# Row-sum reciprocals spread by DMAs through DRAM in place of TensorE transposes, in a two-block transformer kernel

## Chip, cores and metric

One core of one Trainium2 chip runs the whole program in one launch. The metric is the device time of a run in microseconds (us), the median of the runs shown. TensorE is PE in the profile (its weight loads PEld), VectorE is DVE, ScalarE is ACT, GpSimd is POOL, and SyncE, whose queue issues every DMA of this kernel, is SP.

## What is computed

512 tokens of width 1024 pass through two blocks of two layers each. All data are fp32. Every layer of the first block has four attention branches (MLA, stick-breaking, forget-gate "fox", memory), every layer of the second has four others (dense, window with a sink, neighbourhood, differential). A branch has four heads of width 64, and its output is gated. Cut to the part that the change concerns:

```python
def _memory_attention(q, k, v):
    logits = jnp.einsum('bshd,bmhd->bhsm', q * (q.shape[-1] ** -0.5), k)
    p = jax.nn.softmax(logits, axis=-1).astype(v.dtype)
    return jnp.einsum('bhsm,bmhd->bshd', p, v)
...
for n in range(N_BRANCHES):                      # first block
    yb = branches[n].reshape(b, s, BRANCH_WIDTH) * jax.nn.silu(gate_z[:, :, n])
    merged = merged + merge_g[:, :, n] * (yb @ w_branch[n])
out = merged @ w_out
...
mix = jnp.concatenate([o_a * silu(g_a), o_b * silu(g_b), o_c * silu(g_c), o_d * silu(g_d)], axis=-1)
x = x + jnp.einsum('bsm,md->bsd', mix, w_out[l])  # second block
```

Each softmax is divided by the sum of its row, one number for each token and head. Stick-breaking has no such division.

## The kernel before, in words

Projections are kept feature-major: 128 partitions hold features, 512 columns the tokens. Each fp32 matmul is made of three fp32r matmuls on a high and a low part (`mm3`, lines 328 to 330; `split`, lines 319 and 322). Weights come in units of up to 128x1024: one DMA into one of three `raw` buffers (line 376), an ACT copy for the high part, a DVE subtraction for the low one, into three `wh`/`wl` buffers.

Heads are worked in pairs, two heads of 64 features to the 128 partitions. For each head and each block of 128 queries, PE makes the scores (`qk`, lines 512 and 513) and ACT the exponentials with the row sums in `accum_out` (`softmax`, line 534): so a pair's sums stand token-major, as 128 partitions x 2 heads x 4 blocks. PE transposes the probabilities into PSUM (`av`, line 552; the pool of `T` tiles has two buffers), ACT and DVE split them (`th`, `tl`), and PE multiplies by the values (lines 564 and 565) into a feature-major `O`, which `o_evac` (lines 592 and 593) adds into the pair's tile `o`.

The sums are token-major and `o` is feature-major, so the reciprocals have to be turned and spread. Before, `head_rep` does this: a DVE copy (line 617) widens the 128x8 reciprocals to `hrep`, 128x512 with every number 64 times, into a `tmp` buffer; four PE transposes (line 620) turn it into `rep`, 128x512, which takes one of the two `T` buffers in PSUM; DVE multiplies `o` by it (`do_finish`, line 634, or 632 and 636) and then the gate by `o` (line 639).

`recip` (line 652) makes the reciprocals as soon as a pair's second head is done, and `finish` puts the pair on a list, `pending`. The words of `ORDER1` and `ORDER2` say in which order the generators of the branches are advanced, and the word `f` takes the oldest pair off the list and runs `do_finish`. This gives the program's order. The framework's scheduler then orders each engine's instructions anew, within what dependencies and the rotation of buffers allow, so an instruction may stand far from its place in the code. A layer has eight pairs. In the first block six of them have reciprocals (memory, fox, MLA), in the second all eight. Differential attention (`diff_d`) has reciprocals that hold the RMS norm too (line 1417). `dense_a` calls `head_rep` once more for its keys, outside `finish`.

Pairs are finished in this order in the first block: memory 0, memory 1, fox 0, fox 1, MLA 0, MLA 1; in the second: differential 0, dense 0, dense 1, window 0, neighbourhood 0, differential 1, window 1, neighbourhood 1.

SP issues DMAs in its own fixed order and waits at the first that isn't ready. Among them are the weights, and the stacks of queries and keys of each pair (`move`, line 333: `qs`, `ks`, `hs`, `ls`, `kr`), whose parts are copied across partitions before `qk` can read them.

Of the kernel before, what the change touches and what calls it, by code (L numbers as in the profile page):

```python
# [9 lines left out]
F32 = mybir.dt.float32  # L10
# [8 lines left out]
S = 512  # L19
# [265 lines left out]
def half(e):  # L285
    return slice(64 * e, 64 * e + 64)
# [24 lines left out]
class Build:  # L311
# [308 lines left out]
            nc.tensor.transpose(rep[:, cols(tt)], b[:, tt].rearrange("p a b -> p (a b)"), self.ident)  # L620
        return rep

    def finish(self, *args, **kw):
        self.pending.append((args, kw))

    def do_finish(self, at, o, rc=None, g=None, perm=None):

        nc = self.nc
        if rc is not None:
            rep = self.head_rep(rc.rearrange("p e i -> p i e"))  # L630
            if perm:
                nc.vector.tensor_tensor(perm(o), perm(o), rep.rearrange("p (c r) -> p c r", r=8), ALU.mult)
            elif g is None:
                nc.vector.tensor_tensor(o, o, rep, ALU.mult)
            else:
                nc.vector.scalar_tensor_tensor(o, o, g, rep, ALU.mult, ALU.mult)
        self.gated.remove(at)
        self.done.add(at)
        nc.vector.tensor_tensor(self.z[at], self.z[at], o, ALU.mult)
# [16 lines left out]
    def setup(self):  # L656
        nc, tc, ctx = self.nc, self.tc, self.ctx
        pool = lambda n, b, **k: ctx.enter_context(tc.tile_pool(name=n, bufs=b, **k))
        self.cp = pool("const", 1)
        self.psp, self.pss, self.pst, self.pso = (pool(n, b, space=PSUM) for n, b in zip(("psp", "pss", "pst", "pso"), BANKS))  # L660
        self.rawp, self.wp = pool("raw", RAW), pool("wp", WP)
        self.smp = pool("small", 8)
        self.w_done, self.w_ready, self.wout, self.stp = 0, {}, None, None
        self.xs = [nc.dram_tensor(f"xs{i}", (S, DM), F32).ap() for i in range(3)]
        ct = self.cp.tile([128, NCONST], F32, name="ct")
        self.c = {k: ct[:, o : o + n] for k, (o, n) in COFF.items()}
        self.ident = self.c["ident"]
        big = lambda nm: self.cp.tile([128, 8, S], F32R, name=nm)
        self.zth, self.ztl = big("zth"), big("ztl")
        self.zp, self.z = pool("z", ZO), {}  # L670
        self.gated = set()
        nc.scalar.preload_act_table_set(EXPS)
        with tc.tile_pool(name="x0", bufs=1) as xp:
            x = xp.tile([128, 2, 8, 256], F32, name="x0")
            at = 0
            for n, (hf, k0, k1) in enumerate(X0):
                v = x[:, hf, k0:k1]
                c = slice(at, at + 256 * (k1 - k0))
                at = c.stop
                nc.sync.dma_start(v, self.ins["xt"][:, c].rearrange("p (k t) -> p k t", t=256))  # L680
                if n in W0:
                    self.w_prefetch(W0[n])
                self.split(*(t[:, k0:k1, cols(hf, 256)] for t in (self.zth, self.ztl)), v)
        self.w_prefetch(WP)
        nc.sync.dma_start(ct, self.ins["const"])
# [67 lines left out]
    def pools(self, n, st, tmp, pt, p, v):  # L753

        tc = self.tc
        left, right = ExitStack(), ExitStack()
        pool = lambda nm, b: right.enter_context(tc.tile_pool(name=f"{nm}{n}", bufs=b, side="right"))
        self.stp = left.enter_context(tc.tile_pool(name=f"st{n}", bufs=st, side="left"))
        self.pp, self.ptp, self.op, self.vp = pool("p", 1), pool("pt", pt), pool("o", OO), pool("v", v)
        self.tmpp, self.kp = pool("tmp", tmp), pool("k", 1)  # L760
        self.pb = p
        left.callback(lambda: setattr(self, "stp", None))
        return left, right

    def weave(self, order, l, **parts):

        self.pending, self.done = [], set()
        self.mcos = self.msin = self.qm = self.qs = self.krs = self.logf = self.vb = None
        parts = {k: iter(f(l)) for k, f in parts.items()}
        for word in order.split():  # L770
            name = word.rstrip("0123456789")
            for _ in range(int(word[len(name) :] or 1)):
                if name == "f":
                    args, kw = self.pending.pop(0)
                    self.do_finish(*args, **kw)
                else:
                    next(parts[name])
        assert not self.pending
        for name, p in parts.items():
            assert next(p, self) is self, name  # L780


    def layer1(self, l):
        left, right = self.pools(l, **POOLS1)
        with right:
            self.weave(ORDER1, l, first=self.first, mem=self.memory, sb=self.stick, mla=self.mla, misc=self.misc, fox=self.fox, g=self.gates1)
# [444 lines left out]


    def layer2(self, l):
        if 0 not in self.layers and l == self.layers[0] % 2:
            self.constants()
        if l == 0:
# [114 lines left out]
    def diff_d(self, l):  # L1351
# [34 lines left out]
        for pr in range(2):  # L1386
            ku = [unit(hl[2], cols(2 * pr + c, 32), (0, 1, 0, 1)) for c in range(2)]
            o, sm = self.new_o(), self.sums()
            for e in range(2):
# [16 lines left out]
                if e:  # L1406
# [8 lines left out]
                    nc.vector.tensor_scalar(v, v, RMS_EPS, None, ALU.add)  # L1415
                    rs = self.rsqrt(v.rearrange("p a b -> p (a b)")).rearrange("p (a b) -> p a b", a=2)
                    nc.vector.tensor_tensor(rc, rc, rs, ALU.mult)
                    self.finish(6 + pr, o, rc, g)
                yield

    def neigh_c(self, l):
# [59 lines left out]
```

## Time and profile before

| | |
|---|---|
| median of 3 runs | 1417.88 us (1415.82 to 1418.38) |
| the profiled execution | 1419.11 us, of which its span is 1417.3 us |
| PE busy | 1363.2 us, 96% of the span |
| DVE, ACT busy | 999.9 us (71%), 832.3 us (59%) |
| granted PE clock, mean | 0.986 of full speed |
| DMA packets' share of 16 engines | 37.8%, mean 113 GB/s |

The profile is one execution on the chip. A page gives busy times by engine, the chain of waits that ended last, and the costliest groups of instructions; a timeline gives single instructions with the idle time before them in brackets, with what ended it. An idle engine costs nothing unless it bounds the stage. A PE row's duration holds the drain of its pipeline, so what a row costs PE is read from its start to the next row's start.

### The profile page before, as it was taken

The page shows a single profiled execution, that of the slowest core. Times are in us where ns is not written, and L with a number is a line of the kernel's source. Part 1 is how long each engine was busy: PE and PEld are TensorE (multiplying, and loading weights), DVE is VectorE, ACT ScalarE, POOL GpSimd, SP SyncE. Part 2 cuts the span into 40 slices and gives each one's busy share as a digit, 9 for nine tenths or more (in the row PEclk, how much of TensorE's full clock was granted, in tenths as well). Part 3 has the DMA queues.
Part 4 walks back from the last instruction along what each step waited for, and adds up shares of the span by engine and source line. Part 5 has one row for each costly group of instructions (what it writes and reads, how often), then busy time and mean ns, then how long its engine had stood idle before and what let it go on. Part 6 is the DMA issues. An engine that isn't in the chain of part 4 may idle for free.

```text
span 1417.3 us, 20005 instructions
## 1 busy us (share of the span) xinstructions
PE 1363.2 (96%) x7112; PEld 1111.0 (78%) x7112; DVE 999.9 (71%) x2077; ACT 832.3 (59%) x1672; POOL 4.3 (0%) x12
## 2 busy tenths in 40 slices
PE   8999998999999999998999999999999999999998
PEld 7887786777789777877777788877777888877776
DVE  6666545898764776257989675887777575886785
ACT  5584547765413765476856243776866346667763
POOL 0000000000000000000000000000000000000000
PEclk9999999999999999999999999999999999999999
DMA  7534222213625424222135436323434265215241
GB/s 238 172 105 118 72 75 80 75 60 108 207 100 159 139 71 117 75 81 80 41 89 179 163 115 180 111 60 103 131 100 145 109 177 150 75 45 151 62 140 67
DMA packets 61266, 160.31 MB, mean 113 GB/s; under 512 B 11056, under 2 KB 11696, under 8 KB 61168
## 3 DMA queue, kind: packets, MB, share of 16 engines
q1 hardware_dynamic: 61168, 159.05, 37.8%
q8 instruction: 56, 0.92, 0.3%
q14 instruction: 42, 0.34, 0.1%
HBM read 117.92 MB, written 8.91 MB: 89 GB/s over the span
## 4 chain that ended last, share of the span: by engine, by line
PE 77%; ACT 8%; DVE 8%; DMA 4%; issue 2%; SPq 0%; DVEq 0%; ACTq 0%
PE proj L328 11%; PE proj L329 11%; PE proj L330 11%; PE T L552 3%; PE pso L328 3%; PE pso L329 3%; PE pso L330 3%; PE O L564 3%; PE O L565 2%; PE s L901 2%; PE projv L329 2%; PE projv L330 2%; PE projv L328 2%; PE projwb L329 2%; PE projwb L330 2%
## 5 line engine op out<-in xcount | busy, mean ns | idle before, releaser
L328 PE MATMUL proj<-zth,wh 128*128 128x512 f32 (+1 forms) x864 | 323.9, 375 | 9.5 <-ACT wh L319 5.8
L329 PE MATMUL proj<-ztl,wh 128*128 128x512 f32 (+1 forms) x864 | 323.4, 374 | 0.3
L330 PE MATMUL proj<-zth,wl 128*128 128x512 f32 (+1 forms) x864 | 322.9, 374 | 0.0
L322 DVE TENSOR_TENSOR wl<-raw,wh 128x1024 fp32r<-128x1024 f32 (+2 forms) x153 | 183.1, 1197 | 135.1 <-ACT wh L319 126.7
L319 ACT CAST wh<-raw 128x1024 fp32r<-128x1024 f32 (+2 forms) x153 | 157.6, 1030 | 170.4 <-PE proj L329 139.7
L328 PEld LDWEIGHTS proj<-zth,wh 128*128 128x128 f32 x864 | 164.1, 190 | 32.9 <-ACT wh L319 5.8
L330 PEld LDWEIGHTS proj<-zth,wl 128*128 128x128 f32 x864 | 164.2, 190 | 23.7 <-DVE wl L322 1.0
L329 PEld LDWEIGHTS proj<-ztl,wh 128*128 128x128 f32 x864 | 164.3, 190 | 22.8 <-DVE ztl L322 0.7
L322 DVE TENSOR_TENSOR tl<-T,th 128x512 fp32r<-128x512 f32 (+3 forms) x176 | 98.9, 576 | 28.3 <-ACT th L319 27.7
L552 PE MATMUL T<-ct,p 128*128 128x128 f32 x560 | 103.6, 279 | 9.9 <-ACT p L534 7.7
L319 ACT CAST th<-T 128x512 fp32r<-128x512 f32 (+3 forms) x176 | 85.5, 498 | 41.8 <-PE T L552 39.0
L552 PEld LDWEIGHTS T<-ct,p 128*128 128x128 f32 x560 | 71.1, 142 | 30.5 <-ACT p L534 11.3
L528 DVE TENSOR_REDUCE nm<-s 128x1 f32<-128x512 f32 (+1 forms) x128 | 77.5, 616 | 19.6 <-PE s L513 10.2
L534 ACT ACTIVATE p<-s,nm 128x512 f32<-128x512 f32 (+1 forms) x96 | 59.1, 619 | 17.3 <-DVE nm L528 16.7
L564 PE MATMUL O<-th,V 128*128 128x512 f32 (+3 forms) x176 | 62.4, 371 | 2.6 <-ACT th L319 2.2
L565 PE MATMUL O<-tl,V 128*128 128x512 f32 (+3 forms) x160 | 59.3, 376 | 5.0 <-DVE tl L322 4.8
L328 PE MATMUL pso<-wout,zth 128*128 128x512 f32 x128 | 51.7, 404 | 4.7 <-DVE y L1134 4.7
L328 PE MATMUL projv<-wh,zth 128*128 128x256 f32 (+1 forms) x192 | 55.0, 287 | 0.0
L330 PE MATMUL projv<-wh,ztl 128*128 128x256 f32 (+1 forms) x192 | 54.7, 285 | 0.0
L329 PE MATMUL projv<-wl,zth 128*128 128x256 f32 (+1 forms) x192 | 54.6, 284 | 0.0
L330 PE MATMUL projwb<-y,wl 128*128 128x512 f32 x128 | 51.6, 403 | 0.0
L328 PE MATMUL projwb<-y,wh 128*128 128x512 f32 x128 | 51.1, 399 | 0.2
(380 smaller groups left out, 2927.7 us busy)
## 6 DMA issues: line engine op xcount, KB each, us to landing
raw<-in_w_dram SPq DMA_DIRECT2D x173, 512.0 KB
xs<-y SPq DMA_DIRECT2D x12, 512.0 KB
ks<-hs SPq DMA_DIRECT2D x32, 128.0 KB
early<-xs SPq DMA_DIRECT2D x16, 256.0 KB
bias<-in_bias_dram SPq DMA_DIRECT2D x8, 448.0 KB
qs<-hs SPq DMA_DIRECT2D x24, 128.0 KB
qs<-ls SPq DMA_DIRECT2D x24, 128.0 KB
hs<-ls SPq DMA_DIRECT2D x24, 128.0 KB
```

What stands on the lines that cost most here:

```text
L319: self.nc.scalar.copy(h, src)
L322: self.nc.vector.tensor_tensor(l, src, h, ALU.subtract)
L328: self.nc.tensor.matmul(ps, ah, bh, start=i == 0, stop=False)
L329: self.nc.tensor.matmul(ps, ah, bl, start=False, stop=False)
L330: self.nc.tensor.matmul(ps, al, bh, start=False, stop=i == n - 1)
L528: nc.vector.tensor_reduce(nm, s, AX.X, ALU.max, negate=True)
L534: nc.scalar.activation(p[:, :w], src, AF.Exp, bias=nm, scale=sc, accum_out=sm)
L552: nc.tensor.transpose(T[:, cols(a)], P[i][:, c : c + 128], self.ident)
L564: nc.tensor.matmul(o[:, c], vsel(j), th[:, c], start=j == 0, stop=False)
L565: nc.tensor.matmul(o, vsel(j), tl[:, :w], start=False, stop=j == nk - 1)
L901: nc.tensor.matmul(z[:, c:w], m, x, start=False, stop=n == len(sums) - 1, skip_group_check=True)
```

## The change

`finish` counts the pairs that a layer still has to come. For all but the last one of a layer in the first block (`late = 1`) and the last two in the second (`late = 2`), if they have reciprocals, it issues three DMAs on SP at once: one writes the 128x8 reciprocals to a new DRAM tensor of 2x4x128, token order last (so each of the 1,024 numbers is a piece of four bytes), and two read a head's 512 numbers back, each row spread over 64 partitions, into `rep`, now an SBUF tile of a new pool of two buffers (`repp`). `do_finish` multiplies by this tile; the DVE copy and the four transposes are not made. 22 of the 28 pairs with reciprocals take this way: five in each layer of the first block, six in each of the second. The other six, and the keys of `dense_a`, keep `head_rep`.

```diff
-    def finish(self, *args, **kw):
-        self.pending.append((args, kw))
-
-    def do_finish(self, at, o, rc=None, g=None, perm=None):
+    def finish(self, at, o, rc=None, **kw):
+
+        self.to_finish -= 1
+        if rc is not None and self.to_finish >= self.late:
+            d = self.nc.dram_tensor(f"rc{self.nrc}", (2, 4, 128), F32).ap()
+            self.nrc += 1
+            with self.nc.allow_non_contiguous_dma(reason="few bytes"):
+                self.nc.sync.dma_start(d.rearrange("e i p -> p e i"), rc)
+            rep = self.repp.tile([128, S], F32, tag="rep", name="rep")
+            for e in range(2):
+                self.nc.sync.dma_start(rep[half(e)], d[e].rearrange("i p -> (i p)").partition_broadcast(64))
+            kw["rep"] = rep
+        self.pending.append(((at, o, rc), kw))
+
+    def do_finish(self, at, o, rc=None, g=None, perm=None, rep=None):
 
         nc = self.nc
         if rc is not None:
-            rep = self.head_rep(rc.rearrange("p e i -> p i e"))
+            if rep is None:
+                rep = self.head_rep(rc.rearrange("p e i -> p i e"))
...
-        self.tmpp, self.kp = pool("tmp", tmp), pool("k", 1)
+        self.tmpp, self.kp, self.repp = pool("tmp", tmp), pool("k", 1), pool("rep", 2)
...
-        self.pending, self.done = [], set()
+        self.pending, self.done, self.to_finish = [], set(), 8
...
     def layer1(self, l):
+        self.late = 1
...
     def layer2(self, l):
+        self.late = 2
```

Since `rep` no longer waits for a buffer of `T` and of `tmp`, the scheduler sets the multiplications elsewhere. Three places follow. Each comes twice in the program, once for each layer of its block, and the engine's rows are those of the first layer.

DVE, first block, memory attention, between the reciprocals of pair 0 and the low parts (`tl`) of pair 1's last head; before:

```order
L652 RECIPROCAL sums<-sums 128x8
L593 TENSOR_TENSOR o<-O,ot 64x512
L322 TENSOR_TENSOR tl<-T,th 128x512
L528 TENSOR_REDUCE nm<-s 128x1
L322 TENSOR_TENSOR tl<-T,th 128x512
L528 TENSOR_REDUCE nm<-s 128x1 x2
L593 TENSOR_TENSOR o<-O,ot 64x512
L322 TENSOR_TENSOR tl<-T,th 128x512 x2
L322 TENSOR_TENSOR wl<-raw,wh 128x1024
```

The same place now:

```order
L664 RECIPROCAL sums<-sums 128x8
L593 TENSOR_TENSOR o<-O,ot 64x512
L322 TENSOR_TENSOR tl<-T,th 128x512
L528 TENSOR_REDUCE nm<-s 128x1
L322 TENSOR_TENSOR tl<-T,th 128x512
L528 TENSOR_REDUCE nm<-s 128x1 x2
L593 TENSOR_TENSOR o<-O,ot 64x512
L646 TENSOR_TENSOR o<-o,rep 128x512
L322 TENSOR_TENSOR tl<-T,th 128x512 x2
L651 TENSOR_TENSOR z<-z,o 128x512
```

The multiplication by `rep` came much later before (after the fox rows and most of the stick-breaking); now it stands right behind the pair's last addition, ahead of two `tl` that PE needs.

DVE, second block, differential attention, behind the last step of pair 0's reciprocals (the first row); before:

```order
L1417 TENSOR_TENSOR sums<-sums,rs_y 128x8
L528 TENSOR_REDUCE nm<-s 128x1
L1402 TENSOR_SCALAR rl<-rl,nlam,sums 128x1
L528 TENSOR_REDUCE nm<-s 128x1
L1403 SCALAR_TENSOR_TENSOR p<-p_9412,rl,p 128x512
L322 TENSOR_TENSOR wl<-raw,wh 128x1024
L1401 RECIPROCAL rl<-s_9427 128x1
L528 TENSOR_REDUCE nm<-s 128x1
L1402 TENSOR_SCALAR rl<-rl,nlam,sums 128x1
L528 TENSOR_REDUCE nm<-s 128x1
L1403 SCALAR_TENSOR_TENSOR p<-p_9429,rl,p 128x512
L1401 RECIPROCAL rl<-s_9444 128x1
```

The same place now:

```order
L1431 TENSOR_TENSOR sums<-sums,rs_y 128x8
L528 TENSOR_REDUCE nm<-s 128x1
L1416 TENSOR_SCALAR rl<-rl,nlam,sums 128x1
L528 TENSOR_REDUCE nm<-s 128x1
L1417 SCALAR_TENSOR_TENSOR p<-p_9397,rl,p 128x512
L322 TENSOR_TENSOR wl<-raw,wh 128x1024
L1415 RECIPROCAL rl<-s_9412 128x1
L528 TENSOR_REDUCE nm<-s 128x1
L1416 TENSOR_SCALAR rl<-rl,nlam,sums 128x1
L528 TENSOR_REDUCE nm<-s 128x1
L1417 SCALAR_TENSOR_TENSOR p<-p_9414,rl,p 128x512
L648 SCALAR_TENSOR_TENSOR o<-o,subg,rep 128x512
```

Again the multiplication moved forward, to ten rows behind the reciprocals and ahead of the next softmax work of the same branch.

SP, first block, the stacks of fox's second pair; before:

```order
L333 DMA qs<-ls 64x512
L376 DMA raw<-in_w_dram 128x1024
L333 DMA hs<-ls 64x512
L333 DMA ls<-cqrows 4x512
L333 DMA ls<-hs 64x512
L333 DMA kr<-ckrows 4x512
L333 DMA kr<-ls 64x512
L333 DMA ks<-hs 64x512 x2
```

The same place now, with the DMAs of fox's first pair among them:

```order
L333 DMA qs<-ls 64x512
L376 DMA raw<-in_w_dram 128x1024
L630 DMA rc<-sums 128x8x1
L333 DMA hs<-ls 64x512
L333 DMA ls<-cqrows 4x512
L333 DMA kr<-ls 64x512
L633 DMA rep<-rc 64x512 x2
L333 DMA ls<-hs 64x512
L333 DMA kr<-ckrows 4x512
L333 DMA ls<-ckrows 4x512
L333 DMA ks<-hs 64x512 x2
```

The write waits for the reciprocals and the two reads wait for the write, and the stacks of the next pair stand behind both.

## Rows read from the trace of the kernel before

**Rows 1.** Page, part 1: busy time, share of the span, instructions.

```profile
PE 1363.2 (96%) x7112; PEld 1111.0 (78%) x7112; DVE 999.9 (71%) x2077; ACT 832.3 (59%) x1672; POOL 4.3 (0%) x12
```

**Rows 2.** Page, part 4: the chain that ended last, by engine.

```profile
PE 77%; ACT 8%; DVE 8%; DMA 4%; issue 2%; SPq 0%; DVEq 0%; ACTq 0%
```

**Rows 3.** Groups by line and form: busy us, mean ns, idle before and releasers.

```profile
L634 DVE TENSOR_TENSOR o<-o,rep 128x512 f32<-128x512 f32 x20 | 13.7, 683 | 6.1 <-PE rep L620 5.5
L617 DVE COPY hrep<-sums 128x512 f32<-128x512 f32 x28 | 11.6, 420 | 0.1
```

**Rows 4.** Timeline of PE: start us, duration us, instruction [idle before <- releaser].

```profile
157.09 0.50 PE L328 MATMUL proj<-zth,wh 128*128 128x512 f32 x1 [1.50 <-DVE cql L932]
...
278.81 0.63 PE L620 MATMUL rep<-ct,hrep 128*128 128x128 f32 x4
279.28 0.60 PE L552 MATMUL T<-ct,p 128*128 128x128 f32 x4
...
1014.12 0.60 PE L620 MATMUL rep<-ct,hrep 128*128 128x128 f32 x4
1014.47 0.36 PE L512 MATMUL s<-ks,qs 128*128 128x256 f32 x1
```

**Rows 5.** Timeline of PE, two pairs finished together in the second block.

```profile
1044.28 1.07 PE L620 MATMUL rep<-ct,hrep 128*128 128x128 f32 x8
1045.89 0.44 PE L552 MATMUL T<-ct,p 128*128 128x128 f32 x2 [0.54 <-DVE o L634]
1046.83 0.41 PE L552 MATMUL T<-ct,p 128*128 128x128 f32 x1 [0.51 <-DVE o L632]
...
1048.59 0.58 PE L565 MATMUL O<-tl,V 128*128 128x256 f32 x1 [0.70 <-DVE tl L322]
```

**Rows 6.** Busy us by stretch: length, PE, PEld, DVE, ACT, POOL, PEclk, DMA, GB/s.

```profile
1040.00:1060.00 20.00, 17.33 (x94) 13.69 (x92) 16.04 (x44) 11.31 (x29) 0.00 (x0) 0.83 0.42 111
1336.00:1356.00 20.00, 17.24 (x98) 13.69 (x97) 16.32 (x44) 11.97 (x31) 0.00 (x0) 0.91 0.46 141
```

**Rows 7.** Timeline of DVE behind the memory branch's first reciprocals.

```profile
96.36 0.19 DVE L652 RECIPROCAL sums<-sums 128x8 f32<-128x8 f32 x1
...
101.27 0.68 DVE L593 TENSOR_TENSOR o<-O,ot 64x512 f32<-64x512 f32 x1 [0.91 <-ACT ot L592]
102.87 1.29 DVE L322 TENSOR_TENSOR tl<-T,th 128x512 fp32r<-128x512 f32 x2 [0.91 <-ACT th L319]
```

**Rows 8.** Timeline of PE, the first reader of these `tl`.

```profile
103.92 0.39 PE L565 MATMUL O<-tl,mV 128*128 128x512 f32 x1
```

**Rows 9.** Timeline of DVE behind the differential branch's first reciprocals.

```profile
931.27 0.15 DVE L1417 TENSOR_TENSOR sums<-sums,rs_y 128x8 f32<-128x8 f32 x1
...
935.94 0.75 DVE L1403 SCALAR_TENSOR_TENSOR p<-p,rl,p 128x512 f32<-128x512 f32 x1
...
938.40 0.74 DVE L1403 SCALAR_TENSOR_TENSOR p<-p,rl,p 128x512 f32<-128x512 f32 x1
```

**Rows 10.** Timeline of PE, the reader of the last of these `p`.

```profile
939.85 0.38 PE L552 MATMUL T<-ct,p 128*128 128x128 f32 x2
```

**Rows 11.** Timeline of SP's DMA issues: start us, us on the queue.

```profile
80.55 1.11 SPq L333 DMA_DIRECT2D ks<-hl  x2
...
83.46 0.47 SPq L333 DMA_DIRECT2D hl<-hl  x1
...
226.05 0.46 SPq L333 DMA_DIRECT2D hs<-ls  x1
...
238.16 0.49 SPq L333 DMA_DIRECT2D hs<-hs  x1
```

**Rows 12.** The chain that ended last, in order of time: start us, us, what.

```profile
992.80 4.77 DMA hs<-hs
```

**Rows 13.** Page, part 3: DMA queue, packets, MB, share of 16 engines' time.

```profile
q1 hardware_dynamic: 61168, 159.05, 37.8%
```

**Rows 14.** The same view of 113.5 to 118.5 us, only small DMAs in flight.

```profile
q1 hardware_dynamic: 244, 0.02, 3.2%
```

More of the change, by code (lines that the diff above doesn't have):

```diff
@@ L670, in setup @@
         self.zp, self.z = pool("z", ZO), {}
-        self.gated = set()
+        self.gated, self.nrc = set(), 0
         nc.scalar.preload_act_table_set(EXPS)
@@ L1417, in diff_d @@
                     nc.vector.tensor_tensor(rc, rc, rs, ALU.mult)
-                    self.finish(6 + pr, o, rc, g)
+                    self.finish(6 + pr, o, rc, g=g)
                 yield
```

## The prediction

> **What bounds the kernel now.** I read the views from the whole down to the place. Part 1 of the page shows PE busy for 96% of the span, DVE for 71% and ACT for 59% [rows 1]; the chain of waits that ended last runs through PE for 77%, with ACT and DVE at 8% each [rows 2]. So a microsecond taken off PE's row of instructions comes off the time, one taken off DVE does not, and a microsecond that PE is made to wait goes onto it. The groups by line give the price of a finished pair on DVE: a copy of 0.42 us and a multiplication of 0.683 us [rows 3]. The group's idle time shows that nearly all that DVE waited for there came from the transposes (5.5 of 6.1 us) [rows 3]. The timelines of PE and DVE then show each place, and SP's issues show when a transfer may start.
>
> The sum goes against the profiled execution, 1419.11 us. The median of the runs shown is 1417.88 us, 1.23 us lower, and I take that off at the end. A change under 0.2%, some 2.8 us, can't be told from none.
>
> **What is removed.** Four transposes for a pair are printed as 0.60 to 0.63 us long, but what they cost PE is the time from their start to the next row's start: 279.28 - 278.81 = 0.47 us and 1014.47 - 1014.12 = 0.35 us [rows 4]; I take the mean, 0.41 us. The 22 pairs go, less two: the group of memory pair 1 in each layer stands shortly before a place where PE idles 1.50 us for DVE's `cql` [rows 4], so what is won ahead of it is lost at it. 20 x 0.41 = **8.2 us** off PE (7.0 to 9.4 by the two rows).
>
> The 22 copies are 22 x 0.42 = 9.2 us of DVE work [rows 3]. I cost them at nothing: PE's work covers DVE's, and if that cover were gone they would be a gain. The multiplication now reads two operands from SBUF rather than one from PSUM; `p`, made from SBUF on the same shape, takes 0.74 to 0.75 us [rows 9] against 0.683 [rows 3], at most 1.5 us of DVE's time over 22 pairs and, covered likewise, also nothing.
>
> **What moves.** In one stretch of the second block two pairs were finished together. Their two `rep` took both `T` buffers, so the next transposes of probabilities had to wait until DVE had multiplied: PE idles 0.54 and 0.51 us for `o`, then 0.70 us for the late `tl` [rows 5]. With `rep` in SBUF the `T` buffers stay free and two of the three waits have no cause; the third comes of the lateness that the first two made. The place comes once in each layer, so 2 x 1.75 = 3.5 us. The granted clock in the two stretches is 0.83 and 0.91 of full speed [rows 6]: full speed is the higher of PE's two levels (2.4 GHz, the lower is 1.2), so part of each stretch ran at the lower, and PE had idled before. At the full clock the stretches could be shorter by up to 0.17 x 20 = 3.4 and 0.09 x 20 = 1.8 us, 5.2 us together. That the clock fell because of just these waits is not shown, so I take half, 2.6 us. Together **6.1 us** (3.5 to 8.7).
>
> **What is added.** Three DMAs a pair, 66 in all. Their reads deliver 22 x 0.26 = 5.8 MB to the 159 MB of the queue, which fills 37.8% of the 16 engines' time [rows 13]; I cost the bandwidth at nothing. An issue of such a transfer holds SP about 0.5 us [rows 11], 33 us over the program, spread over 22 places.
>
> The cost that counts is a wait. DVE runs in order, and the multiplication now stands 5 us or so behind the reciprocals, ahead of work that PE needs. Let L be the time from the reciprocals to the landing of both reads. It is a write, two issues and a read in a row. No row shows such a chain, so it is bounded. From below: a read pair of the same size is issued at 80.55, its second half half-way through the 1.11 us, so at 81.10; its reader is issued at 83.46 [rows 11], so a transfer has landed after 2.36 us at most. Two of them and the second read's issue make 2.36 + 0.59 + 2.36 = **5.3 us**. From above: behind a load of weights a like transfer took 4.77 us [rows 12], so 4.77 + 0.59 + 4.77 = **10.1 us**. The write in 1,024 pieces of four bytes has no row: small packets took 0.032 x 5 us x 16 / 244 = 10 ns of an engine each [rows 14], the mean packet 0.378 x 1417 us x 16 / 61168 = 140 ns [rows 13], so 64 pieces on each of 16 engines are 0.7 to 9 us. I take 1.7 us on top of the lower end, **L = 7.0 us**: the places have no weight load issued right ahead, and the pieces resemble the small packets far more than those of 2 KB.
>
> DVE's cover at two places. Memory pair 0: reciprocals done at 96.36 + 0.19 = 96.55, the addition ahead of the multiplication at 101.27 + 0.68 = 101.95, 5.4 us later [rows 7]. The two `tl` behind it end their first half at about 103.52 [rows 7], and PE reads it at 103.92 [rows 8]: 0.4 us of slack. Differential pair 0: 931.42 to 936.69, 5.3 us [rows 9]; the next `p` ends at 939.14 and PE reads it at 939.85 [rows 9, 10]: 0.7 us of slack. So PE loses L - 5.8 and L - 6.0 us there. At 7.0 that is 1.2 + 1.0, twice over for the layers, 4.4 us. The other nine places of a pair of layers have 12 to 23 rows of DVE work between reciprocals and multiplication in the order now, against 7 and 10 at these two; I put half as much again on them, an estimate that no row gives. In all **6.6 us**; written with L, 1.5 x 2 x (2L - 11.8) = 6L - 35.4 us above L = 5.9, and nothing below.
>
> **The sum:** -8.2 - 6.1 + 6.6 = -7.7, so 1411.4 us profiled and **1410.2 us** as a median. Best end: -9.4 - 8.7 and no stall, 1399.8 us. Worst end: -7.0 - 3.5 + (6 x 10.1 - 35.4 = 25.2) = +14.7, 1432.6 us.
>
> **Rivals.**
>
> *DVE held in line by the write, slower.* The place is the multiplication ahead of `tl` and `p`, the price 6L - 35.4, and it decides from L = 8.3 us, where it eats the 14.3 us won. At L = 9.5 it costs 21.6 us: +7.3, 1425.2 us. For it: the pieces, of which the trace has no like, and 4.77 us for a transfer that met weights [rows 12]. Against: small packets are cheap [rows 14]. The Trainium skill's page "DMA: Bandwidth & Descriptors", section "Rules for kernel authors", speaks against this change: a strided last dimension becomes one descriptor for each element and should be rearranged to be contiguous. By that rule the write is 1,024 descriptors; how long they take, no run here shows. Chance 0.20.
>
> *The chain lands in time, better.* If the write is as quick as any other transfer, L is 5.3 us, below 5.4 and 5.9: no stall, -14.3, 1403.6 us. For it: the lower bound is itself a ceiling on a transfer, since its reader was issued after both halves [rows 11]. Against: 1,024 pieces. The same page, section "Anatomy of one DMA — SWDGE (gpsimd) path", puts the fixed cost of a DMA at about 2.0 us, most of it the receipt of the write, which is heaviest for HBM. An estimate from that page would be 2.0 + 0.6 + 2.0 = 4.6 us for L and so no stall, though these DMAs are issued by SP, and the row's 2.36 us is the measurement that I use. Chance 0.16.
>
> *SP's queue.* The write waits at the head of SP for its reciprocals, and the stacks of the next pair stand behind it. In fox `hs<-ls` went out at 226.05 and `hs<-hs` at 238.16 [rows 11]; fox's first reciprocals lie between. If the later pair's scores start 3 us late in each layer, the loss is 6 us: -1.7, 1416.2 us. Against: SP was free for long between these issues. Chance 0.12.
>
> *The gain is not realised.* The two stretches keep their waits, since `tl` or the weights are late there anyway: -8.2 + 6.6 = -1.6, 1416.3 us. Chance 0.10.
>
> That the change does not do what it says is out: SP's order has 22 writes and 22 pairs of reads, and PE keeps the transposes of six pairs and two sets of keys only.
>
> **How the numbers follow.** The forecast has the rest, 0.42. Forecast and better case make 0.58 for faster by over 0.2%; SP's queue and the gain not realised lie within it, 0.22; slower has 0.20. The range begins at the best end, rounded to 1400 us, and ends at 1425 us, with the middle of the slower rival: half of that rival, 0.10, lies above, and I leave out little below. It holds both signs; the forecast's own, with L from 6.2 to 7.8 us, is 1405 to 1415 us.
>
> **What would show it.** Right: the transposes' count falls from 120 to 32; the idle PE time at the two stretches goes and their granted clock rises to about 1.0; the multiplication waits on DVE for the DMA of `rep` 1 to 2 us at memory pair 0 and differential pair 0, and PE then waits for `tl` and `p` about a microsecond. The landing of `rep` minus the end of the reciprocals is L, and tells forecast, slower and better case apart at 5.9 and 8.3 us. Wrong: multiplications that never wait, or that wait several microseconds; PE idle for scores behind fox's or the second block's stacks; a granted clock that falls at new places, as a stall of PE may bring; the stretches at 1040 and 1336 us unchanged.

## The result, and the profile after

The changed kernel takes 1568.13 us (median of 4 runs, 1566.84 to 1571.88) against 1417.09 us of the kernel before in the same session: a ratio of 1.1065, 95% interval 1.1044 to 1.1086. It is 151 us slower; 1410.2 us was forecast, and the range ended at 1425. The profiled execution took 1571.88 us.

Part 1 of the page (busy us, share of the span, instructions), against [rows 1]; the queue's row of part 3, against [rows 13]; and part 4, the chain that ended last, by engine and by line, against [rows 2]:

```profile
PE 1391.3 (89%) x7024; PEld 1133.7 (72%) x7024; DVE 994.9 (63%) x2055; ACT 828.9 (53%) x1672; POOL 4.3 (0%) x12
...
q1 hardware_dynamic: 87568, 164.91, 37.2%
...
PE 61%; DMA 22%; DVE 8%; ACT 6%; issue 2%; SPq 1%; DVEq 0%; ACTq 0%
DMA rc<-sums 10%; PE proj L328 9%; PE proj L330 9%; PE proj L329 9%; DMA rep<-rc 3%; DMA hs<-hs 3%; PE pso L328 2%; PE pso L329 2%; PE pso L330 2%; PE T L552 2%; DMA raw<-in_w_dram 2%; DMA ml<-qrl 2%; PE O L565 2%; PE projv L329 2%; PE projv L328 2%
```

The span grew by 1570.1 - 1417.3 = 152.8 us. PE's idle time went from 1417.3 - 1363.2 = 54.1 to 1570.1 - 1391.3 = 178.8 us, 124.7 us more; and PE's busy time rose by 28.1 us although it has 88 matmul instructions fewer. A tenth of the span is now the 4 KB writes `rc` on the chain, where all DMAs together made 4% before. The load of the DMA queue says nothing of it: 37.2% of the span against 37.8%.

Who PE waited for, its largest waits (us in total, times, longest us), after:

```profile
PE O L565 <- DVE tl L322: 39.4, 14, 9.4
PE s L512 <- DMA hs<-hs: 27.4, 5, 7.7
PE T L552 <- DVE p L1417: 25.8, 4, 8.6
PE proj L328 <- DVE cql L945: 17.5, 2, 9.0
PE s L512 <- DVE nm L525: 10.4, 2, 5.5
PE s L330 <- DMA ml<-qrl: 10.2, 4, 5.0
```

Four of these (`tl`, `p`, `cql`, `nm`) are DVE's, two are other DMAs, stacks that have nothing to do with the reciprocals. At `nm` DVE itself waits for another DMA, that of a bias (11.7 us in two waits). The same view before, where `p`, `nm` and `ml` have no entry and `cql` has 3.0 us:

```profile
PE O L565 <- DVE tl L322: 4.8, 7, 1.1
...
PE s L512 <- DMA hs<-hs: 2.4, 2, 1.9
```

The place that the prediction spoke of first, memory pair 0: the timeline of DVE, against [rows 7], then SP's issues and PE, against [rows 8]:

```profile
97.91 0.19 DVE L664 RECIPROCAL sums<-sums 128x8 f32<-128x8 f32 x1
...
102.81 0.69 DVE L593 TENSOR_TENSOR o<-O,ot 64x512 f32<-64x512 f32 x1 [0.91 <-ACT ot L592]
112.28 0.69 DVE L646 TENSOR_TENSOR o<-o,rep 128x512 f32<-128x512 f32 x1 [8.78 <-DMA rep<-rc]
112.89 1.28 DVE L322 TENSOR_TENSOR tl<-T,th 128x512 fp32r<-128x512 f32 x2
```

```profile
98.13 0.38 SPq L630 DMA_DIRECT2D rc<-sums  x1
106.80 2.78 SPq L633 DMA_DIRECT2D rep<-rc  x2
```

```profile
113.62 0.80 PE L565 MATMUL O<-tl,mV 128*128 128x512 f32 x1 [7.56 <-DVE tl L322]
...
116.78 0.63 PE L329 MATMUL proj<-ztl,wh 128*128 128x512 f32 x1
...
118.57 0.39 PE L329 MATMUL proj<-ztl,wh 128*128 128x512 f32 x1
```

The write is issued 0.03 us after the reciprocals end (98.10), and the first read can go out only 8.67 us later; over the 22 writes of the program this step takes 8.6 to 11.8 us (8.7 to 11.3 where SP issues nothing else between). The multiplication starts at 112.28, 112.28 - 98.10 = 14.2 us after the reciprocals; DVE has stood for 8.78 us and PE for 7.56. Then a projection on PE takes 0.63 us in place of 0.39. The stretches say why (length, PE, PEld, DVE, ACT and POOL busy, granted clock, DMA share, GB/s):

```profile
95.00:105.00 10.00, 9.60 (x59) 7.63 (x58) 5.98 (x13) 8.11 (x24) 0.00 (x0) 1.00 0.19 50
113.60:117.60 4.00, 3.98 (x11) 2.77 (x12) 2.90 (x5) 1.48 (x4) 0.00 (x0) 0.50 0.00 0
```

Behind the stall the granted clock is 0.50, the lower level (1.2 GHz), for 4 us, and then full again. Such stretches bring the mean clock from 0.986 to 0.939. Added up over the clock's records in the two traces, PE is busy at the lower level for 121 us, where it was 37 before; at half the clock up to half of the 84 us more is time lost, enough for the 28 us of longer busy time.

Where are the 8.67 us? Part 3 of the page for a stretch in which only such a write was in flight, from 0.17 us behind its issue at 545.73 to just before its reads' issue at 556.81 (the first row has the stretch in 40 slices of 0.27 us, in tenths busy):

```profile
DMA  0017710000000000000000000000000000000000
...
q1 hardware_dynamic: 1040, 0.00, 4.4%
```

All 1,040 packets are through within 1.8 us of the issue. For nine further microseconds no DMA engine shows a packet, and still the write is not reported as landed. So the price is no transfer time: it is behind the last packet, where the busy shares show nothing.

### The profile page after: what moved, and what is told of

Same layout as the page of the kernel before. It is cut to its first block, busy times and chain, and to the rows that moved or that the text cites. A ratio compares the mean times of both kernels' runs of the same rounds, so it can differ in the third digit from the quotient of the medians.

```text
span 1570.1 us, 19874 instructions
## 1 busy us (share of the span) xinstructions
PE 1391.3 (89%) x7024; PEld 1133.7 (72%) x7024; DVE 994.9 (63%) x2055; ACT 828.9 (53%) x1672; POOL 4.3 (0%) x12
## 3 DMA queue, kind: packets, MB, share of 16 engines
q1 hardware_dynamic: 87568, 164.91, 37.2%
## 4 chain that ended last, share of the span: by engine, by line
PE 61%; DMA 22%; DVE 8%; ACT 6%; issue 2%; SPq 1%; DVEq 0%; ACTq 0%
DMA rc<-sums 10%; PE proj L328 9%; PE proj L330 9%; PE proj L329 9%; DMA rep<-rc 3%; DMA hs<-hs 3%; PE pso L328 2%; PE pso L329 2%; PE pso L330 2%; PE T L552 2%; DMA raw<-in_w_dram 2%; DMA ml<-qrl 2%; PE O L565 2%; PE projv L329 2%; PE projv L328 2%
## 5 line engine op out<-in xcount | busy, mean ns | idle before, releaser
L328 PE MATMUL proj<-zth,wh 128*128 128x512 f32 (+1 forms) x864 | 329.9, 382 | 24.2 <-DVE cql L945 17.5
L329 PE MATMUL proj<-ztl,wh 128*128 128x512 f32 (+1 forms) x864 | 329.3, 381 | 0.3
L330 PE MATMUL proj<-zth,wl 128*128 128x512 f32 (+1 forms) x864 | 329.2, 381 | 0.0
L328 PEld LDWEIGHTS proj<-zth,wh 128*128 128x128 f32 x864 | 168.4, 195 | 49.0 <-DVE cql L945 18.0
L330 PEld LDWEIGHTS proj<-zth,wl 128*128 128x128 f32 x864 | 168.2, 195 | 25.3 <-DVE wl L322 1.0
L329 PEld LDWEIGHTS proj<-ztl,wh 128*128 128x128 f32 x864 | 168.6, 195 | 23.9 <-DVE ztl L322 0.8
L552 PE MATMUL T<-ct,p 128*128 128x128 f32 x560 | 109.1, 288 | 28.2 <-DVE p L1417 25.8
L528 DVE TENSOR_REDUCE nm<-s 128x1 f32<-128x512 f32 (+1 forms) x128 | 77.2, 613 | 21.7 <-PE s L513 12.5
L646 DVE TENSOR_TENSOR o<-o,rep 128x512 f32<-128x512 f32 x20 | 13.8, 689 | 84.2 <-DMA rep<-rc 77.5
L565 PEld LDWEIGHTS O<-tl,V 128*128 128x128 f32 x160 | 32.1, 201 | 33.6 <-DVE tl L322 28.7
L592 ACT COPY ot<-O 64x512 f32<-64x512 f32 x48 | 28.0, 582 | 50.7 <-PE O L565 50.1
```

The lines of the kernel that those rows point to most:

```text
L328: self.nc.tensor.matmul(ps, ah, bh, start=i == 0, stop=False)
L329: self.nc.tensor.matmul(ps, ah, bl, start=False, stop=False)
L330: self.nc.tensor.matmul(ps, al, bh, start=False, stop=i == n - 1)
L528: nc.vector.tensor_reduce(nm, s, AX.X, ALU.max, negate=True)
L552: nc.tensor.transpose(T[:, cols(a)], P[i][:, c : c + 128], self.ident)
L565: nc.tensor.matmul(o, vsel(j), tl[:, :w], start=False, stop=j == nk - 1)
```

## The experiments

Theories at the start: **A**, the write in 1,024 pieces takes some 10 us and DVE stands in line behind it; **B**, SP's queue or the transfers behind the write are held up, whatever DVE does; **C**, the new order of the engines' instructions is itself worse. Diffs are against the changed kernel; in e1, e7 and e12 to e14 every compute engine keeps the changed kernel's order of instructions, while in e2 to e5 and in the versions with turned reciprocals the scheduler ordered the program anew. Ratios are to the kernel before, with 95% intervals.

### Fewer pieces: e1_rows32

```diff
-                self.nc.sync.dma_start(d.rearrange("e i p -> p e i"), rc)
+                self.nc.sync.dma_start(d.rearrange("e i p -> (e i p)").rearrange("(p e i) -> p e i", e=2, i=4), rc)
```

> The reciprocals are written as 128 pieces of 32 bytes, not 1,024 of four, into the same 4 KB; the two reads and the order of every compute engine are those of the changed kernel. Left out: the order of the numbers (each token is scaled by another's reciprocal). Theory A (the write in 1,024 pieces takes some 10 us, and DVE stands in line at the multiplication): the read's issue follows the write's by about 3 us instead of 8.7 to 11.3, and the time falls to 1410 to 1450 us. Theory B (SP's queue, where the stacks stand behind a write and two reads that wait, whatever the write takes): the time stays above 1500 us. Theory C (the new order of the engines' instructions is itself worse): above 1500 us, since that order is the same.

Measured: 1410.38 us, ratio 0.9945 (0.9929 to 0.9961). At memory pair 0:

```profile
97.80 0.33 SPq L630 DMA_DIRECT2D rc<-sums  x1
99.20 1.12 SPq L633 DMA_DIRECT2D rep<-rc  x2
```

```profile
97.58 0.19 DVE L664 RECIPROCAL sums<-sums 128x8 f32<-128x8 f32 x1
...
103.21 0.69 DVE L646 TENSOR_TENSOR o<-o,rep 128x512 f32<-128x512 f32 x1
```

1.40 us from issue to issue, and a multiplication that waits for nothing, 5.4 us behind the reciprocals. Not one instruction of the compute engines stands elsewhere than in the changed kernel, and 158 us are gone. C falls; B as it was put (whatever the write takes) falls too. The whole loss hangs on how these writes of 4 KB are laid out.

### The multiplication later: e2_late

```diff
+                after = next(i for i in reversed(nc.cur_bb.bb.instructions) if i.engine == self.dve)
...
+                es.enter_context(self.tc.issue_after(after))
```

> The changed kernel, but each multiplication by rep, and the gate's behind it, is issued on DVE behind the last DVE instruction of the program text ahead of it, so 16 to 93 DVE rows after its reciprocals, where the changed kernel has 8 to 50. The DMAs are the same. Theory A: the write still takes 10 us and is mostly hidden, so 1410 to 1470 us, with the wait of the multiplication for the DMA a tenth of the 107 us of the changed kernel. Theory B: the stacks of the next pair still stand behind the reads on SP, so above 1500 us.

Measured: 1510.00 us, ratio 1.0652 (1.0621 to 1.0683). The time is B's outcome, but neither theory stands alone: DVE's waits for `rep` fell from 106.8 us in 18 waits to 42.1 us in 8, which took 59 us off, and 92 us of loss stay. PE's waits:

```profile
PE s L512 <- DMA hs<-hs: 30.9, 6, 8.1
PE proj L328 <- DVE cql L952: 16.5, 2, 8.3
PE s L330 <- DMA ml<-qrl: 9.3, 3, 5.0
PE O L565 <- DVE tl L322: 9.1, 9, 3.3
```

The wait for `tl` went from 39.4 to 9.1 us, that for the stacks `hs<-hs` did not.

### The DMAs with no reader: e3_unread

```diff
-            kw["rep"] = rep
```

> The three DMAs of each pair are made and nobody reads rep; every pair takes the copy and the four transposes as before. Theory A: no engine waits for the write, so within 1415 to 1440 us. Theory B: SP's stacks and weights stand behind the write and the reads as in the changed kernel, so most of the loss stays, 1500 us or more; PE then waits for hs<-hs as it does there (27 us).

Measured: 1496.53 us, ratio 1.0553 (1.0517 to 1.059), close to B's outcome (1500 us or more). With no compute engine waiting for `rep`, and all the transposes back, the three DMAs alone cost 78 us; SP stands 206 us at the reads, in 22 waits, and PE waits 25.8 us for `hs<-hs`.

### What there is to win: e4_free

```diff
-            d = self.nc.dram_tensor(f"rc{self.nrc}", (2, 4, 128), F32).ap()
...
+            rep = self.one
...
```

> No DMA, no copy, no transposes for the 22 pairs: o is multiplied by a tile of ones that stands in SBUF from the start. Left out: the division by the row sum of these pairs. It prices what spreading can win at the most. Theories A and B: 1400 to 1408 us, the 14.3 us of the sum's first two terms below the 1418 us of before. Theory C: well above 1418 us.

Measured: 1407.91 us, ratio 0.9925 (0.9903 to 0.9948). The spreading as a whole is worth some 10 us, not 14. Part 1 of the page, span 1406.5 us:

```profile
PE 1350.7 (96%) x7024; PEld 1101.5 (78%) x7024; DVE 996.3 (71%) x2055; ACT 828.8 (59%) x1672; POOL 4.8 (0%) x13
```

PE is busy 12.5 us less; it idles 1406.5 - 1350.7 = 55.8 us, 1.7 us more than before. At the first of the prediction's two stretches, some 3 us earlier in this run, PE has none of the three waits left, and the granted clock is full, where it was 0.83 [rows 6]:

```profile
1030.00:1050.00 20.00, 19.52 (x107) 15.74 (x106) 16.96 (x48) 13.41 (x33) 0.00 (x0) 1.00 0.23 60
```

### The write alone: e5_write_only

```diff
-            rep = self.repp.tile([128, S], F32, tag="rep", name="rep")
-            for e in range(2):
-                self.nc.sync.dma_start(rep[half(e)], d[e].rearrange("i p -> (i p)").partition_broadcast(64))
-            kw["rep"] = rep
```

> The copy and the four transposes of before for every pair, and besides the write in 1,024 pieces on SP, which nobody reads or waits for; no reads. Theory B1 (SP stands at the reads until the write has landed, and the stacks with it): without reads SP never stands for the write, so 1415 to 1435 us, and PE waits for hs<-hs no longer than before (2.4 us). Theory B2 (a transfer issued behind the write on the same queue lands no sooner than it): most of the 79 us of the unread DMAs stays, 1470 us or more, and PE waits for hs<-hs some 25 us.

Measured: 1474.68 us, ratio 1.0381 (1.035 to 1.0411): B2. SP never stood for the write, and two thirds of the 78 us are there. SP's issues at one place:

```profile
1085.56 0.38 SPq L630 DMA_DIRECT2D rc<-sums  x1
1085.99 1.24 SPq L333 DMA_DIRECT2D ks<-hs  x1
...
1095.04 0.46 SPq L333 DMA_DIRECT2D hs<-hs  x1
```

The stack `ks<-hs`, issued just behind the write, keeps `hs<-hs`, the move that has to wait for it, back for 9.05 us (1095.04 - 1085.99).

### The write on another queue: e6_write_pool

```diff
-                self.nc.sync.dma_start(d.rearrange("e i p -> p e i"), rc)
+                self.nc.gpsimd.dma_start(d.rearrange("e i p -> p e i"), rc)
```

(and no reads, as in the run before)

> As the run with the write alone, but the write is issued by GpSimd, whose DMAs go through a queue of their own. Theory B2: nothing of SP stands behind the write, so 1415 to 1430 us. If the pieces slow every transfer in flight, on whatever queue, it stays at 1470 us or more. Theory B1: 1415 to 1430 us in this run and in the one before.

Measured: 1476.02 us, ratio 1.0391 (1.0359 to 1.0424). B2 falls in the form in which it was put: the queue doesn't matter. Three engines at one place, GpSimd's issue, SP's issue and PE:

```profile
1080.42 0.89 POOL L630 DMA_DIRECT2D rc<-sums  x1 [24.01 <-DVE tl L322]
```

```profile
1081.39 0.52 SPq L333 DMA_DIRECT2D hs<-hs  x1
```

```profile
1090.95 1.20 PE L512 MATMUL s<-hs 128*128 128x256 f32 x3 [5.31 <-DMA hs<-hs]
```

`hs<-hs`, SBUF to SBUF and on SP's queue, lets PE go on only 9.6 us after its issue, while GpSimd's write is outstanding. In this run PE, DVE, ACT and SP have, row for row, the order of the kernel before, so the 56 us come of the 22 writes alone. The same two rows in the kernel before, 4.33 us apart, and PE waits for nothing:

```profile
1051.58 0.52 SPq L333 DMA_DIRECT2D hs<-hs  x1
```

```profile
1055.91 0.63 PE L512 MATMUL s<-hs 128*128 128x256 f32 x3
```

Whatever is held up, other transfers go through it.

### Twice the bytes in a piece: e7_rows8

```diff
-                self.nc.sync.dma_start(d.rearrange("e i p -> p e i"), rc)
+                self.nc.sync.dma_start(d.rearrange("e i p -> (e i p)").rearrange("(k p j) -> p k j", k=4, j=2), rc.rearrange("p e (h j) -> p (e h) j", j=2))
```

> The changed kernel with the write in 512 pieces of 8 bytes; the order of the compute engines is that of the changed kernel. Left out: the order of the numbers, as in the run with 128 pieces. If the price goes with the number of pieces, the read's issue follows the write's by about (512 - 128) x (10.5 - 1.4) / (1024 - 128) + 1.4 = 5.3 us, and the time is 1440 to 1490 us, under half of the 158 us between 128 and 1,024 pieces, since part of the 5.3 us is hidden. If it is a matter of pieces under some size, the time is that of the changed kernel or that of 128 pieces.

Measured: 1434.76 us, ratio 1.0104 (1.0069 to 1.0138), a little below the expected 1440 to 1490 us. At memory pair 0 the read goes out at 101.90, 4.35 us behind the write at 97.55; over the program 3.1 to 5.9 us. The price is graded; from 9 us to 4 us it loses most of its effect on the time. That the rest is hidden behind other work is the likely reason, and wasn't traced.

### Pieces apart, nobody reads: e9_spread

The write alone again (without reads), but:

```diff
-            d = self.nc.dram_tensor(f"rc{self.nrc}", (2, 4, 128), F32).ap()
+            d = self.nc.dram_tensor(f"rc{self.nrc}", (2, 4, 128, 16), F32).ap()[:, :, :, 0]
```

> The run with the write alone on SP, every instruction in the same order, but each of the 1,024 pieces of four bytes goes to 64 bytes of its own in DRAM. If neighbouring pieces hinder each other (the same few bytes of DRAM written again and again), the write becomes quick and the time falls from 1474.7 us to 1420 to 1435 us. If it is the number of pieces alone, it stays at 1465 to 1480 us.

Measured: 1418.85 us, ratio 0.9999 (0.9983 to 1.0015). The same 1,024 pieces, every engine's instructions in the order of e5, and the loss is gone. The place that was shown for the write alone:

```profile
1044.89 0.38 SPq L630 DMA_DIRECT2D rc<-sums  x1
1045.32 1.32 SPq L333 DMA_DIRECT2D ks<-hs  x1
...
1048.44 0.46 SPq L333 DMA_DIRECT2D hs<-hs  x1
```

3.12 us from `ks<-hs` to the move that waits for it, in place of 9.05. So it is not the number of pieces by itself: it is that they stand side by side in DRAM.

### The same in the changed kernel: e12_dense, e13_spread_read, e14_same_row

Three kernels with one order of instructions that differ in the addresses of the write alone (`W` is what the diff's last line writes to; the reads take 512 numbers in a row each).

```diff
+        self.rcd = nc.dram_tensor("rcd", (22, 16384), F32).ap()
+        nc.sync.dma_start(self.rcd[:, :1024], self.ins["x"][:22])
...
+            d = self.rcd[self.nrc]
...
+                self.nc.sync.dma_start(W, rc)
e12  W = d[:1024].rearrange("(e i p) -> p e i", e=2, i=4)
e13  W = d.rearrange("(e i p j) -> p e i j", e=2, i=4, p=128)[:, :, :, 0]
e14  W = d[:2048].rearrange("(p e i j) -> p e i j", e=2, i=4, p=128)[:, :, :, 0]
```

> Control of the next two runs: the changed kernel, its 22 little arrays of reciprocals as rows of one DRAM tensor, whose first 4 KB are filled once at the start. The write has the same 1,024 pieces side by side. All theories: within 2% of the changed kernel's 1568 us, and the read's issue 9 to 12 us behind the write's.

> The control with every piece of four bytes in 64 bytes of its own; the reads take the first 4 KB of the row as they did, so they still wait for the write, and the order of every engine is the control's. Left out: most of rep's numbers are those of the filling, not reciprocals. If pieces that share 64 bytes hinder each other, and nothing else makes the loss: the read's issue 1.4 to 3 us behind the write's and 1405 to 1430 us. If the number of pieces has a part in it that the write alone didn't show: above 1450 us.

> As the run with pieces spread, but the eight numbers of one partition share 64 bytes (a piece of four bytes every eight), 1,024 pieces as before. Left out: as there. If only pieces of different partitions that share 64 bytes hinder each other (they go out on different DMA engines): 1405 to 1430 us. If any pieces that share 64 bytes do: the wait between write and read is over 5 us and the time above 1450 us.

Measured: e12 1578.82 us, ratio 1.1127 (1.1103 to 1.1152); e13 1414.62 us, 0.9968 (0.9952 to 0.9983); e14 1486.88 us, 1.0479 (1.0458 to 1.05). SP's issues at memory pair 0, in this order:

```profile
97.54 0.38 SPq L630 DMA_DIRECT2D rcd<-sums  x1
108.82 1.12 SPq L633 DMA_DIRECT2D rep<-rcd  x2
```

```profile
97.14 0.38 SPq L630 DMA_DIRECT2D rcd<-sums  x1
99.68 1.12 SPq L633 DMA_DIRECT2D rep<-rcd  x2
```

```profile
97.49 0.61 SPq L630 DMA_DIRECT2D rcd<-sums  x1
104.09 1.14 SPq L633 DMA_DIRECT2D rep<-rcd  x2
```

Always 1,024 pieces of four bytes: 11.28 us from issue to issue when sixteen share 64 bytes, 6.60 when eight do, 2.54 when each has 64 bytes of its own. Over the program it is 9.2 to 12.5, 5.6 to 8.4 and 2.5 to 5.0 us. The pages of e12 and e13 show the same 87,601 packets. Sharing by the numbers of one partition is enough, so it does not take pieces of different partitions. Among pieces that share, their number may have a part: in e7, as in e14, eight share 64 bytes, and its 512 pieces, twice as long, took 4.35 us. Which part of the memory path holds the writes back, whether 64 bytes is the unit, and whether it is sharing or the narrow range of addresses (4, 8 and 64 KB for the whole write), wasn't tried; e1, quick with 128 pieces in 4 KB, says that the range alone is not enough.

### Reciprocals turned first: e8_turned_late, e10_turned, e11_dve_turned, e15_dve_late

Versions with the reference's result whose write has long pieces. e8 and e10:

```diff
-                self.nc.sync.dma_start(d.rearrange("e i p -> p e i"), rc)
+            t = self.pst.tile([128, S], F32, tag="T", name="rct")
+            self.nc.tensor.transpose(t[:8, :128], rc.rearrange("p e i -> p (e i)"), self.ident)
+            rt = self.repp.tile([128, 128], F32, tag="rt", name="rt")
+            self.nc.vector.tensor_copy(rt[:8], t[:8, :128])
+            self.nc.sync.dma_start(d.rearrange("e i p -> (e i) p"), rt[:8])
```

e11 and e15:

```diff
...
+            self.nc.vector.tensor_copy(w[:, :8], rc.rearrange("p e i -> p (e i)"))
+            self.nc.vector.transpose(rt, w)
+            dt = d.rearrange("e i (b q) -> b (e i) q", b=4)
+            for b in range(4):
+                self.nc.sync.dma_start(dt[b], rt[32 * b : 32 * b + 8])
```

e8 and e15 have the late multiplication besides.

> One transpose on TensorE turns the 128x8 reciprocals to 8x128, DVE copies them to SBUF, and the write has 8 pieces of 512 bytes; the reads are those of the changed kernel, and the multiplications stand late, as in the run of that name. Theory A: the read's issue follows the write's by 1.4 to 3 us, no multiplication waits, and the time is that of the tile of ones, 1408 us, with 22 short transposes of 0.1 to 0.3 us on PE: 1410 to 1415 us. If the transposes into one of the two T buffers cost what the four did, 1416 to 1420 us.

> As the run with one transpose and 8 pieces of 512 bytes, but the multiplications stand where the scheduler puts them. If the late multiplications cost that run (1417.3 us) what it lacks to the run with 128 pieces (1410.4 us), it is 1409 to 1414 us; if the transpose and its T buffer do, 1415 to 1420 us.

> DVE turns the reciprocals in blocks of 32x32 in SBUF, and four writes of 8 pieces of 128 bytes bring them to DRAM; no transposes on TensorE for these 22 pairs. Four issues on SP take about 1.9 us, so the last write lands some 3.5 us after the reciprocals and the reads some 4 us later. Theory A: 1408 to 1414 us. If the further issues on SP or three more DVE instructions for each pair cost, 1415 to 1422 us.

> The reciprocals turned by DVE and written in pieces of 128 bytes (four writes a pair), with the multiplications late; the reference's result. Theory: no transposes for 22 pairs, no wait for rep: 1408 to 1416 us, below both kernels. If the other order of the instructions gives it back as in the runs with turned reciprocals: 1417 to 1428 us.

Measured: e8 1417.30 us, ratio 0.9989 (0.9969 to 1.0009); e10 1433.52 us, 1.0097 (1.0068 to 1.0126); e11 1427.15 us, 1.006 (1.0035 to 1.0084); e15 1422.65 us, 1.0026 (1.0015 to 1.0037). None is faster than the kernel before, and e10 and e11 lie above all that was expected of them, though DVE's waits for `rep` are down to 5.7 us in e10, 1.4 in e8 and 1.1 in e11. In e10 PE stands for the reciprocals themselves:

```profile
PE rct L630 <- DVE sums L1434: 5.9, 2, 3.0
```

The rest was not traced to a place: each of these lets the scheduler order the program anew, and four kernels with nearly the same work lie 16 us apart. That is more than the 10 us to be won, and it is also how far the parts of the loss that e2, e3 and e4 give can be off.

## Why the prediction was wrong

**The write's price, the step that failed.** L was taken as 7.0 us, between 5.3 and 10.1; it is 14.2 us at memory pair 0 and, at differential pair 0, where the multiplication starts at 1023.54 behind reciprocals that ended at 1008.73, 14.8:

```profile
1008.58 0.15 DVE L1431 TENSOR_TENSOR sums<-sums,rs_y 128x8 f32<-128x8 f32 x1
...
1023.54 0.75 DVE L648 SCALAR_TENSOR_TENSOR o<-o,subg,rep 128x512 f32<-128x512 f32 x1 [9.54 <-DMA rep<-rc]
```

At memory pair 0 the write has 8.7 us of it, above the 4.77 of its high end and about twice the 2.36 + 1.7 of the forecast. The reads have 112.28 - 106.80 = 5.5 us with both issues, as the high end had it (0.59 + 4.77), but more than the forecast's 0.59 + 2.36. So the write was the larger error, and the reads the smaller. The prediction priced a piece by the time of its packet [rows 14], and that was near: the packets are through in 1.8 us. But a write is over when it is reported as landed, and no row of before had pieces side by side in DRAM. Its high end was also not what its own numbers gave: 9 us for the pieces at 140 ns each [rows 13] belonged in it, 2.36 + 9 + 0.59 + 4.77 = 16.7 us. That end would have held L, though not the time: with 6 x 16.7 - 35.4 = 64.8 us of stalls the worst end is some 1472 us. And the move at 83.46 [rows 11] that it calls the reader overwrites what the pair has read; the bound of 2.36 us is the same.

**Descriptors and the report of the landing.** The Trainium skill's page "DMA: Bandwidth & Descriptors", section "Rules for kernel authors", says to keep the last dimension contiguous: right in its advice, worth 158 us here (e1). A descriptor for each element, which it gives as the reason, is not by itself what costs here: 1,024 pieces spread out take 2.54 us to the next issue and the time of before (e13). Its section "Anatomy of one DMA — SWDGE (gpsimd) path" says that a DMA's semaphore waits until the write is confirmed as landed: the trace fits that, with nine idle microseconds behind the last packet, though not with about 2 us for them, and e6's median of 10.6 us is on that very path. What the nine microseconds are spent on no trace shows.

**DVE's line.** The mechanism was as described: wait at `rep`, then PE at `tl` and `p` (7.56 and 8.64 us, against 8.4 and 8.8 by L - 5.8 and L - 6.0 at the measured L):

```profile
1026.45 0.69 PE L552 MATMUL T<-ct,p 128*128 128x128 f32 x2 [8.64 <-DVE p L1417]
```

The formula gives 6 x 14.5 - 35.4 = 52 us. PE's waits for `tl`, `p` and `cql` are 82.7 us, against 7.8 before, 75 us more. The runs give much the same, if the parts simply add: 151 - 78 = 73 us on top of the unread DMAs, near 83 when the 10 us are added that the changed kernel saves on transposes; the late multiplication gets back 59 us of it (e2). What was too small is the half as much again for the other places. Memory pair 1 (`cql`, 17.5 us) and MLA's first pair (9.4 and 8.4 of the 39.4 us of `tl`) stall PE as long as the two places that were priced: the 18 and 20 DVE rows that lie between there cover less than the 15 to 16 us that L takes there, and of DVE's 106.8 us at `rep` the two priced places, with both layers, have 35.7.

**Other transfers, the term that was missing.** The prediction had a rival in which stacks are late because SP stands, at 6 us and 0.12. Its cause was too narrow: the write alone, for which SP does not wait, costs 54 us (e5, 0.0381 x 1420.3 us of before in its session); the reads, at which SP does stand, some 24 more (e3, 0.0553 x 1417.7 = 78 in all). While the write is outstanding, transfers land late on its own queue (e5) and on another one (e6). In the changed kernel PE's waits for `hs`, `ml` and, through the bias, `nm` are 48.0 us, against 2.4 before. The sum cost the new DMAs' effect on all others at nothing, by their bytes.

**The clock.** The sum had it as a gain only, at the two stretches; that a stall may bring it down at new places stood among the signs of being wrong, without a price. While PE stood at memory pair 0, and for 4 us behind it, the clock was granted at 0.50; PE's busy time rose by 28 us over the program, a fifth of the whole loss, where the fewer transposes should have lowered it.

**What was right.** The transposes did go; the row of the tile `rep` in the changed kernel has 32 in place of 120:

```profile
L620 PE MATMUL rep<-ct,hrep x32: 271/272/302, 343.0 to 1522.6; 128*128 128x128 f32 x32
```

Without the write the sum without stalls was of the right kind and too high: 14.3 us were expected of the removed transposes and the two stretches, 10 came (e4), with an interval of some 7 to 14. PE's busy time fell by 12.5 us, at least the 8.2 of the transposes. At the first stretch the waits went and the clock rose to 1.00, as forecast; so the rival of the gain not realised, in which the waits stay there, does not hold at that place. But PE's idle time over the program did not fall, so the 3.5 us came back elsewhere, in places that weren't traced.

**The rivals.** The slower one had the right sign, the right place and one half of the cause, and a price of 7.3 us instead of 151, for want of a bound on L, of the other places and of every effect on other transfers.

## What to carry to other kernels

A DMA that writes token-major numbers into a feature-major row of DRAM in four-byte pieces is not priced by its bytes or its packets: look at the next issue that waits for it. Before such a write is put into a program, run it once with its pieces contiguous and once spread apart, results aside; here two such runs (e1 and e13) showed that the whole loss hung on how 4 KB are laid out. And where an in-order engine is set to wait for a DMA, ask besides who else has transfers in flight in that time.

## What the runs showed of the hardware that had not been expected

- 1,024 four-byte pieces written side by side: 8.6 to 11.8 us to the issue that waits for them, over the program, while the packets are through 1.8 us after the write's issue (one place). At memory pair 0 it is 6.60 us with eight to 64 bytes, 2.54 us with one to 64 bytes and 1.40 us with 128 pieces of 32 bytes; 512 pieces of 8 bytes take 3.1 to 5.9 us over the program.
- While such a write is outstanding, a 64x512 move within SBUF on another queue is through after 9.6 us (e6), where 4.33 us are enough without the write; one on the same queue, behind it, makes its successor wait 9.05 us (e5), where 3.12 do with the pieces apart (e9).
- GpSimd's queue shows 704 packets for 22 writes, 32 each of 128 bytes, and its median from issue to landing is 10.6 us all the same: larger packets in the profile went with the same price here.

```profile
q0 software_dynamic: 704, 0.09, 0.6%
...
rc<-sums POOLq DMA_DIRECT2D x22, 4.0 KB, 10.6
```
